# A hybrid decoder layer on one core: first weights through other tiles and in one chain, and the norm of the linear attention in four VectorE operations a piece

## The chip, the core and the metric

The kernel runs on one core of one Trainium2 chip. The metric is device time in microseconds (us). The engines are TensorE (PE; PEld is its weight load), VectorE (DVE), ScalarE (ACT), GpSimd (POOL) and SyncE (SP), which here issues every DMA. Each engine works through its own list of instructions in order and waits on semaphores where an operand or a buffer is not ready.

## What is computed

The reference is one decoder layer for 1024 tokens of width 1024. Cut to what matters here:

```python
h = rmsnorm(x, norm_mix)
proj = h @ w_in          # q, kv, gates of the sparse attention; q, k, v, rank, r of the linear one; merge gates
k_cmp, v_cmp = compress_blocks(...)
o_a = nsa_attention(...)                         # compressed, selected and sliding-window branches
o_b = gla_chunked(q_gla * GLA_DK ** -0.5, k_gla, v_gla, log_a)
o_b = rmsnorm(o_b, gla_norm)                     # over the 128 values of each head
o_b = o_b * silu(r_gla)
merged = gate_a * (o_a @ w_up_nsa) + gate_b * (o_b @ w_up_gla)
x = x + merged @ w_out
x = x + (silu(rmsnorm(x) @ w_ffn_gate) * (rmsnorm(x) @ w_ffn_up)) @ w_ffn_down
return rmsnorm(x, norm_final)
```

`rmsnorm(x, g)` is `x * rsqrt(mean(x*x) + 1e-6) * g`.

## The kernel before

Everything is kept transposed: 128 features on the partitions, tokens along the row, in halves of 512 tokens. Each float32 operand is split into a high and a low part, and each product is three matmuls (high by high, high by low, low by high). A weight's split has two steps: ACT copies it to the high part (`wh`, L353), then another engine subtracts (`wl`, L354; POOL for the projections' weights).

PE's order is the order in which the program is written. The other engines' lists are set by a scheduler with its own estimate of time, from priorities and from which buffers are free; DMAs of the first loads are kept in the order written (`load`, L481).

**The first stretch.** For each of eight blocks `k` of 128 features the loop from L484 loads both halves of `xT` and the weights `w_s` (queries and half of the keys of the linear attention). These weights pass through the tile `wf`, of which there are two, and which every later weight of the projections uses too. ACT makes `hh`, the high part of the scaled input (L498), DVE the low part `hl` (L501). ACT squares the input in place (L508) and POOL adds the squares up in `ssq` (L510, six times); DVE adds the last block (L527). ACT and DVE split that sum into `ssh` and `ssl` (L530, L531). PE meanwhile does the products of all eight blocks into six PSUM banks, two of them of the tag `m` (L365 to L367). ACT then copies these two banks out as `qg` (L542), which frees them, and PE goes on with the second half of the keys, job `w_t[3]`, in the tag `m` (L404). After its first two blocks comes `first_roots` (L544): four matmuls with `ssh` and `ssl`, then the reciprocal root `rbc`. The jobs of the compressed keys and values follow (`work = dense([j0, ...])`, L710); the weights of job `n+1` are loaded while job `n` runs.

**The norm of the linear attention** (from L945) comes later, in eight pieces of one head and 512 tokens. SP loads the piece `tz`; ACT squares it and takes the high part (L953, L954), POOL the low part (L955). PE sums over the partitions with `onesr`, a tile of ones (L967). `rms_root` (L424) then runs ACT's Ln and Exp (L427, L429) beside four DVE operations (L428, L430, L431, L432), and two more DVE operations apply the gain and `silu(r)` (L971, L972). Between pieces PE works off the query jobs and one gate job from the `fill` queue; their banks of the tag `m` (two) are freed by DVE's `scaled` (L524).

Of the kernel before, what the change touches and what calls it, by code (L numbers as in the profile page):

```python
# [10 lines left out]
F32 = mybir.dt.float32  # L11
F32R = mybir.dt.float32r
BF = mybir.dt.bfloat16
U8 = mybir.dt.uint8
AF = mybir.ActivationFunctionType
OP = mybir.AluOpType
# [223 lines left out]
def layer_kernel(ctx, tc, a, outT):  # L240
# [33 lines left out]
    def ps_t():  # L274
        return bank("t")
# [12 lines left out]
    def big(nm, dt=F32, shape=(1024,)):  # L288
        return sb.tile([128, *shape], dt, name=nm, tag="c", bufs=NBIG)
# [28 lines left out]
    cmul = mcst.tile([128, 64], F32, name="cmul")  # L318
    ones = cst.tile([128, 128], F32, name="ones")
    onesr = cst.tile([128, 128], F32R, name="onesr")  # L320
    identb = mcst.tile([128, 128], BF, name="identb")
    mdb = mcst.tile([128, 128], BF, name="mdb")
    meb = mcst.tile([128, 128], BF, name="meb")
# [7 lines left out]
    def load_consts():  # L331
        load(ident, a["consts"][:, CI:CI + 128])
        load(tri, a["consts"][:, CTRI:CTRI + 128])
        load(cmul, a["consts"][:, CMUL:CMUL + 64])
        load(ggain, a["gla_norm"])
        load(w2b, a["gla_w2b"])
        V.tensor_copy(identb, ident)
        t = big("cst1")
        load(t[:, :768], a["consts"][:, CMD:CMD + 768])
        V.tensor_copy(mdb, t[:, 0:128])  # L340
        V.tensor_copy(meb, t[:, 128:256])
        V.tensor_copy(cmb.rearrange("p b n -> p (b n)"), t[:, 256:768])
        t = big("cst2")
        load(t[:, :64 * NLV], a["consts"][:, CLEV:CLEV + 64 * NLV])
        V.tensor_copy(lev.rearrange("p b n -> p (b n)"), t[:, :64 * NLV])


    def part(src, wh, wl, eng=None, wf=None):

        n = src.shape[1]  # L350
        wf = (wpool.tile([128, 512], F32, name="wf", bufs=2) if wf is None else wf)[:, :n]
        SP.dma_start(wf, src)
        S.activation(wh, wf, AF.Copy)  # L353
        (eng or V).tensor_tensor(wl, wf, f(wh), OP.subtract)  # L354

    def half_weights(src, o):

        n = min(4, src.shape[1] - o)
        wh = wpool.tile([128, 4, 128], F32R, name="wh", bufs=3)
        wl = wpool.tile([128, 4, 128], F32R, name="wl", bufs=3)  # L360
        part(*[t.rearrange("p a b -> p (a b)") for t in (src[:, o:o + n, :], wh[:, :n, :], wl[:, :n, :])], eng=P)
        return wh, wl

    def three(ps, wh, wl, xh, xl, first, last):
# [4 lines left out]
    def dense(jobs, two=True, per=1, ready=None):  # L369

        w, out = dict(ready or {}), []

        def load(n, o):
            if n < len(jobs) and o < jobs[n][0].shape[1] and (n, o) not in w:
                w[n, o] = half_weights(jobs[n][0], o)

        def at(n):
            def getw(k):  # L380
                wh, wl = w[n, k // 4 * 4]
                return wh[:, k % 4, :], wl[:, k % 4, :]
            return getw

        out += [(0.0, lambda: load(0, 0)), (0.0, lambda: load(0, 4))]
        for n in range(len(jobs)):
            items = jobs[n][1](at(n))
            cut = (len(items) // 2 if two else 0) + 4 * per
            out.append((0.0, lambda n=n: load(n + 1, 0)))
            out += items[:cut]  # L390
            out.append((0.0, lambda n=n: load(n + 1, 4)))
            out += items[cut:]
        return out
# [30 lines left out]
    def rms_root(st, n, denom, r, tmp=None):  # L424

        v, q = [t[:, :n] for t in tmp or (tiny("nv", 32), tiny("nq", 32))]
        S.activation(q, st[:, :n], AF.Ln, scale=1.0 / denom, bias=eps)  # L427
        V.tensor_scalar(v, st[:, :n], -0.5 / denom, -0.5 * EPS, op0=OP.mult, op1=OP.add)  # L428
        S.activation(q, q, AF.Exp, scale=-0.5)  # L429
        V.tensor_mul(v, v, q)  # L430
        V.tensor_mul(v, v, q)  # L431
        V.scalar_tensor_tensor(r, v, 1.5, q, op0=OP.add, op1=OP.mult)  # L432
# [21 lines left out]
    def log_exp():  # L454

        tc.keep_in_program_order(S.preload_act_table_set("natural_log_exp_and_others"))
# [7 lines left out]
    V.memset(ones, 1.0)  # L464
    V.memset(eps, EPS)
    V.tensor_copy(onesr, ones)
    log_exp()

    warm = prob("warm", BF)[:, :512]
# [14 lines left out]
    for k in range(NK):  # L484
        if k % 2 == 0:
            wh2, wl2 = big("w0h", F32R, (2, 512)), big("w0l", F32R, (2, 512))
        xf, wf = big("xf"), wpool.tile([128, 512], F32, name="wf", bufs=2)[:, :384]
        th, tl = row("hh", F32R), row("hl", F32R)
        wh, wl = wh2[:, k % 2, :384], wl2[:, k % 2, :384]
        with tc.high_priority():  # L490
            load(xf[:, hs(0)], a["xT"][:, k, hs(0)])
            if k == 0:
                load(gains, a["gains"])
            load(wf, a["w_s"][:, k, :])
            load(xf[:, hs(1)], a["xT"][:, k, hs(1)])
            for hf in range(2):
                x, hi = xf[:, hs(hf)], th[:, hs(hf)]
                S.activation(hi, x, AF.Copy, scale=gains[:, 0, k:k + 1])  # L498
                if hf == 0:
                    S.activation(wh, wf, AF.Copy)  # L500
                V.scalar_tensor_tensor(tl[:, hs(hf)], x, gains[:, 0, k:k + 1], f(hi), op0=OP.mult, op1=OP.subtract)  # L501
                if hf == 0:
                    (P if k > 1 else V).tensor_tensor(wl, wf, f(wh), OP.subtract)
        w0.append((wh, wl))
        if k == 0:
            S.activation(ssq, xf, AF.Square)
        else:
            S.activation(xf, xf, AF.Square)  # L508
            if k < NK - 1:
                P.tensor_add(ssq, ssq, xf)  # L510
        hh.append(th)
        hl.append(tl)
    load_consts()
    hhf = [[t[:, hs(hf)] for t in hh] for hf in range(2)]
    hlf = [[t[:, hs(hf)] for t in hl] for hf in range(2)]
# [4 lines left out]
    def scaled(dst, ps, hf, s=None):  # L520
        if s is None:
            V.tensor_mul(dst, ps, rbc[:, hs(hf)])
        else:
            V.scalar_tensor_tensor(dst, ps, s, rbc[:, hs(hf)], op0=OP.mult, op1=OP.mult)  # L524
# [33 lines left out]
    def proj(evac, bank=ps_m, fine=False):  # L558

        def make(getw):  # L560
            out = []
            for hf in range(2):
                out += products(getw, bank, hhf[hf], hlf[hf], 0,
                                lambda p, hf=hf: evac(p, hf), fine)
            return out
        return make

    fill = Fill()
    work = dense([(a["w_t"][3], proj(lambda p, hf: scaled(kg[hf][:, 1, :], p, hf)))])
    fill.add(work[:5] + [(900.0, first_roots)] + work[5:] + [(400.0, root_turned)])  # L570
    fill.flush()


    kc = mcst.tile([128, NG, 2, 64], F32, name="kc")
# [86 lines left out]
    def key_job(br):  # L661
        def evac(p, hf):
            if hf == 0:
                ks[br] = [big(f"ks{br}{g}", F32R) for g in range(NG)]
            rc, rs = mid("rc"), mid("rs")
            SP.dma_start(rc, a["rope"][:, 0, hs(hf)])
            SP.dma_start(rs, a["rope"][:, 1, hs(hf)])
            kt, sw = mid("krt"), mid("ksw")
            scaled(kt, p, hf)
            V.stream_shuffle(sw, kt, swap)  # L670
            V.tensor_mul(kt, kt, rc)
            V.tensor_mul(sw, sw, rs)
            V.tensor_add(kt, kt, sw)
            for g in range(NG):
                r, o = slice(64 * g, 64 * g + 64), slice(64 - 64 * g, 128 - 64 * g)
                k = ks[br][g]
                S.activation(k[r, hs(hf)], kt[r, :], AF.Copy)
                V.tensor_tensor(k[o, hs(hf)], kt[r, :], f(k[r, hs(hf)]), OP.subtract)
        return a["w_t"][6 + br], proj(evac)
# [16 lines left out]
    def token_proj(parts, ncol, evac, after={}):  # L696
        for b in range(NB):
# [6 lines left out]
            for fn in after.get(b, []):  # L704
# [2 lines left out]
    j0, h0, t0, s0 = compress_job(0)  # L707
    j1, h1, t1, s1 = compress_job(1)
    lb, wb = token_weights(a["w_b"], 512, 2)
    work = dense([j0, key_job(0), j1, key_job(1)])  # L710
    fill.add(work[:30] + h0 + work[30:41] + t0 + work[41:45] + s0 + work[45:51] + lb[:1] + work[51:56] + lb[1:2] + work[56:66]
             + h1 + lb[2:] + work[66:])
    fill.flush()

    vs = [big(f"vs{i}", F32R, (2, 4, 128)) for i in range(4)]
# [244 lines left out]
    for n, (h, hf) in enumerate(pieces):  # L960
        if n + 1 < len(pieces):
            ahead.append(squares(*pieces[n + 1]))
        fill.run(4400)
        tz, *parts = ahead.pop(0)
        ps = ps_t()
        for i, t in enumerate(parts):
            PE.matmul(ps, onesr, t, start=i == 0, stop=i == 1)  # L967
        nv, nq = mid("nv"), mid("nq")
        rms_root(ps, 512, float(GDV), nq, [nv, nq])
        t = tz[:, 0, :]  # L970
        V.scalar_tensor_tensor(t, t, ggain, nq, op0=OP.mult, op1=OP.mult)  # L971
        V.tensor_mul(t, t, tz[:, 1, :])  # L972
        SP.dma_start(ob2[:, h, hs(hf)], t)
# [764 lines left out]
```

## Time and profile before

| | before |
|---|---|
| three runs | 1654.77, 1650.31, 1653.8 us (median 1653.8) |
| the profiled execution | 1651.47 us, of which the span is 1649.6 us |
| PE busy | 1583.9 us (96%) |
| DVE, ACT, POOL busy | 1070.0, 809.7, 752.0 us |

The span runs from the first to the last instruction. A matmul's row shows its length in the pipeline; the next one starts before it ends. "[4.71 <-ACT qg L542]" behind a row means that the engine stood idle for 4.71 us before it and that ACT's instruction at L542 ended the wait. In the window rows the granted clock of PE is a share of full speed: 1.00 is 2.4 GHz, 0.50 is 1.2 GHz.

### The profile page before, as it was taken

How to read it: one execution, taken by the hardware profiler on the slowest of the kernel's cores; microseconds unless marked ns; L12 is line 12 of the kernel's file. 1: busy time of each engine (PE TensorE's matmuls, PEld its weight loads, DVE VectorE, ACT ScalarE, POOL GpSimd, SP SyncE). 2: the span in 40 equal slices, each digit the busy share in tenths (PEclk: the TensorE clock that was granted, in tenths of full speed). 3: DMA queues.
4: the chain of work that ended last, by engine and by line, in shares of the span. 5: the costliest groups of instructions: out<-in, count | busy, mean ns of one | idle time of the engine just before them, and what ended most of it. 6: DMA issues, size and time to landing. Idle time of an engine off the chain costs nothing.

```text
span 1649.6 us, 23202 instructions
## 1 busy us (share of the span) xinstructions
PE 1583.9 (96%) x8079; PEld 1314.8 (80%) x8079; DVE 1070.0 (65%) x1759; ACT 809.7 (49%) x1633; POOL 752.0 (46%) x668
## 2 busy tenths in 40 slices
PE   9899999998999999998898989999999999999997
PEld 6788978876888878886777778888888888888886
DVE  7771487695777787778655476744444444489776
ACT  6231466543676666767644344433334333444542
POOL 6210376664234442345124450356665666545560
PEclk9999999999999999999999999999999999999999
DMA  5331212342111111113256551333332333595414
GB/s 175 116 105 46 72 61 74 114 140 74 43 45 43 58 46 42 45 43 103 85 175 212 195 170 45 102 101 108 119 102 97 101 103 102 209 378 153 142 47 144
DMA packets 107208, 178.82 MB, mean 108 GB/s; under 512 B 11969, under 2 KB 26706, under 8 KB 107090
## 3 DMA queue, kind: packets, MB, share of 16 engines
q1 hardware_dynamic: 103778, 171.30, 31.7%
q10 hardware_dynamic: 3312, 6.03, 1.0%
q8 instruction: 64, 1.05, 0.3%
q14 instruction: 54, 0.44, 0.1%
HBM read 129.84 MB, written 47.45 MB: 107 GB/s over the span
## 4 chain that ended last, share of the span: by engine, by line
PE 75%; DVE 9%; DMA 5%; issue 4%; ACT 4%; POOL 3%; SPq 0%; DVEq 0%; ACTq 0%; POOLq 0%
PE m L404 11%; PE m L1352 9%; PE m L1353 9%; PE d L404 9%; PE m L1354 9%; PE m L1667 4%; PE m L1668 4%; PE m L1669 4%; PE t L1133 3%; PE o L1142 3%; PE s L1055 2%; PE s L1056 2%; POOL wl L354 1%; DMA wf<-in_w_out 1%; DVE qs L1004 1%
## 5 line engine op out<-in xcount | busy, mean ns | idle before, releaser
L354 POOL TENSOR_TENSOR wl<-wf,wh 128x512 fp32r<-128x512 f32 x106 | 145.6, 1375 | 319.0 <-ACT wh L353 297.8
L1352 PE MATMUL m<-xt,wh 128*128 128x512 f32 x412 | 161.4, 392 | 2.6 <-ACT sc L1358 2.6
L1354 PE MATMUL m<-xt,wl 128*128 128x512 f32 x412 | 160.3, 389 | 0.0
L1353 PE MATMUL m<-xt,wh 128*128 128x512 f32 x412 | 160.3, 389 | 0.0
L1284 POOL TENSOR_TENSOR wl<-ws,wh 128x512 fp32r<-128x512 f32 x76 | 107.4, 1418 | 91.0 <-ACT wh L1283 71.6
L1111 DVE TENSOR_TENSOR ptl<-t,pth 128x512 fp32r<-128x512 f32 (+1 forms) x168 | 99.5, 597 | 47.4 <-ACT pth L1110 46.0
L1284 POOL TENSOR_TENSOR wl<-wr,wh 128x512 fp32r<-128x512 f32 x69 | 92.4, 1339 | 57.9 <-ACT wh L1283 56.9
L353 ACT ACTIVATE wh<-wf 128x512 fp32r<-128x512 f32 x106 | 66.4, 628 | 98.7 <-PE m L404 38.9
L1283 ACT ACTIVATE wh<-wr 128x512 fp32r<-128x512 f32 x87 | 54.9, 631 | 120.4 <-POOL wl L1284 84.0
L404 PE MATMUL m<-hh,wh 128*128 128x512 f32 x240 | 103.8, 433 | 10.0 <-DVE qr L524 5.3
L1284 POOL TENSOR_TENSOR wl<-wd,wh 128x512 fp32r<-128x512 f32 x56 | 82.4, 1474 | 61.5 <-ACT wh L1283 58.0
L1667 PE MATMUL m<-xb,wh 128*128 128x512 f32 x280 | 109.3, 390 | 0.0
L1669 PE MATMUL m<-xb,wl 128*128 128x512 f32 x280 | 108.9, 389 | 0.0
L1668 PE MATMUL m<-xb,wh 128*128 128x512 f32 x280 | 108.9, 389 | 0.0
L1110 ACT ACTIVATE pth<-t 128x512 fp32r<-128x512 f32 (+1 forms) x168 | 87.6, 526 | 38.4 <-PE t L1133 35.3
L1284 DVE TENSOR_TENSOR xb<-ar,xb 128x512 fp32r<-128x512 f32 (+1 forms) x84 | 81.3, 984 | 35.2 <-ACT xb L1283 35.2
L1283 ACT ACTIVATE wh<-ws 128x512 fp32r<-128x512 f32 x76 | 47.9, 630 | 111.9 <-PE m L1353 95.2
L404 PE MATMUL m<-hh,wl 128*128 128x512 f32 x240 | 95.8, 399 | 1.1 <-POOL wl L354 1.1
L404 PE MATMUL m<-hl,wh 128*128 128x512 f32 x240 | 95.8, 399 | 0.0
L1352 PEld LDWEIGHTS m<-xt,wh 128*128 128x128 f32 x412 | 77.3, 188 | 22.2 <-ACT sc L1358 6.4
L1133 PE MATMUL t<-ident,p 128*128 128x128 f32 x528 | 83.6, 275 | 11.2 <-DVE ptl L1111 10.0
L1354 PEld LDWEIGHTS m<-xt,wl 128*128 128x128 f32 x412 | 77.3, 188 | 16.2
(381 smaller groups left out, 4674.1 us busy)
## 6 DMA issues: line engine op xcount, KB each, us to landing
ar<-actd SPq DMA_DIRECT2D x70, 256.0 KB, 3.0
wf<-in_w_t SPq DMA_DIRECT2D x58, 256.0 KB, 2.8
wr<-in_w_gate SPq DMA_DIRECT2D x44, 256.0 KB, 2.6
wr<-in_w_upf SPq DMA_DIRECT2D x44, 256.0 KB, 2.7
zd<-zt SPq DMA_DIRECT2D x40, 256.0 KB, 2.0
wd<-in_w_down SPq DMA_DIRECT2D x33, 256.0 KB, 5.2
wf<-in_w_out SPq DMA_DIRECT2D x32, 256.0 KB, 3.2
actd<-t SPq DMA_DIRECT2D x30, 256.0 KB, 2.5
```

The costliest lines, as they stand in the source:

```text
L354: (eng or V).tensor_tensor(wl, wf, f(wh), OP.subtract)
L404: PE.matmul(st["p"], w, x, start=k + i == 0, stop=k == n - 1 and i == 2)
L1111: V.tensor_tensor(tl[:, :c], pt[:, :c], f(th[:, :c]), OP.subtract)
L1133: PE.transpose(pt[:, bs(2 * b + par)], self.p[par][:, bs(kb + b)], ident)
L1283: S.activation(th, src, AF.Copy)
L1284: eng.tensor_tensor(tl, src, f(th), OP.subtract)
L1352: PE.matmul(ps, wh[:, c], xh, start=first and k == 0, stop=False, skip_group_check=not first)
L1353: PE.matmul(ps, wh[:, c], xl, start=False, stop=False, skip_group_check=not first)
L1354: PE.matmul(ps, wl[:, c], xh, start=False, stop=k == MH - 1, skip_group_check=not first)
L1667: PE.matmul(dst, wh[:, c], xh, start=first and p == 0, stop=False, skip_group_check=not first)
L1668: PE.matmul(dst, wh[:, c], xl, start=False, stop=False, skip_group_check=not first)
L1669: PE.matmul(dst, wl[:, c], xh, start=False, stop=p == NP - 1, skip_group_check=not first)
```

## The change

Four things change. The weights `w_s` pass through `ws`, a tile of the pool of ten middle tiles. The two halves of the weights of job `w_t[3]` are loaded by the same ordered list as the first loads, right after them and ahead of the constants. That job is put at the head of the chain of jobs that follows, with `first_roots` and `root_turned` (L552) at the same places in PE's order. And the norm of the linear attention uses a tile `meanr` of -1/128, so that the bank holds minus the mean; ACT takes Ln, Exp and a Square, and DVE four operations.

```diff
+    meanr = mcst.tile([128, 128], F32R, name="meanr")
...
-    def part(src, wh, wl, eng=None, wf=None):
+    def part(src, wh, wl, eng=None, wf=None, dma=SP.dma_start):
...
-        SP.dma_start(wf, src)
+        dma(wf, src)
...
+    V.tensor_scalar(meanr, ones, -1.0 / GDV, None, op0=OP.mult)
...
-        xf, wf = big("xf"), wpool.tile([128, 512], F32, name="wf", bufs=2)[:, :384]
+        xf, wf = big("xf"), mid("ws")[:, :384]
...
+    first = {(0, o): half_weights(a["w_t"][3], o, load) for o in (0, 4)}
     load_consts()
...
-    work = dense([(a["w_t"][3], proj(lambda p, hf: scaled(kg[hf][:, 1, :], p, hf)))])
-    fill.add(work[:5] + [(900.0, first_roots)] + work[5:] + [(400.0, root_turned)])
-    fill.flush()
...
-    work = dense([j0, key_job(0), j1, key_job(1)])
-    fill.add(work[:30] + h0 + work[30:41] + t0 + work[41:45] + s0 + work[45:51] + lb[:1] + work[51:56] + lb[1:2] + work[56:66]
-             + h1 + lb[2:] + work[66:])
+    work = dense([(a["w_t"][3], proj(lambda p, hf: scaled(kg[hf][:, 1, :], p, hf))), j0, key_job(0), j1, key_job(1)], ready=first)
+    fill.add(work[:5] + [(900.0, first_roots)] + work[5:20] + [(400.0, root_turned)] + work[20:48] + h0 + work[48:59] + t0
+             + work[59:63] + s0 + work[63:69] + lb[:1] + work[69:74] + lb[1:2] + work[74:84] + h1 + lb[2:] + work[84:])
...
-            PE.matmul(ps, onesr, t, start=i == 0, stop=i == 1)
+            PE.matmul(ps, meanr, t, start=i == 0, stop=i == 1)
         nv, nq = mid("nv"), mid("nq")
-        rms_root(ps, 512, float(GDV), nq, [nv, nq])
+        S.activation(nq, ps, AF.Ln, scale=-1.0, bias=eps)
+        S.activation(nq, nq, AF.Exp, scale=-0.5)
+        S.activation(nv, nq, AF.Square, scale=float(np.sqrt(0.5)))
+        V.scalar_tensor_tensor(nv, ps, EPS, nv, op0=OP.subtract, op1=OP.mult)
+        V.scalar_tensor_tensor(nq, nv, 1.5, nq, op0=OP.add, op1=OP.mult)
```

How the lists move. On POOL at the end of the first stretch, before (`w0l` is the low part of the last `w_s`, `ssq` the last sum of squares, `wl` the weights of `w_t[3]` and what follows):

```order
L510 TENSOR_TENSOR ssq<-ssq,xf 128x1024
L503 TENSOR_TENSOR w0l<-wf,w0h 128x384
L510 TENSOR_TENSOR ssq<-ssq,xf 128x1024
L354 TENSOR_TENSOR wl<-wf,wh 128x512 x7
L630 MEMSET hd 128x256
```

and now:

```order
L512 TENSOR_TENSOR ssq<-ssq,xf 128x1024
L505 TENSOR_TENSOR w0l<-ws,w0h 128x384
L355 TENSOR_TENSOR wl<-wf,wh 128x512 x2
L512 TENSOR_TENSOR ssq<-ssq,xf 128x1024
L355 TENSOR_TENSOR wl<-wf,wh 128x512 x5
L630 MEMSET hd 128x256
```

Two `wl`, those of `w_t[3]`, moved ahead of the last sum of squares. On ACT at the same place, before (`wh` is a weight's high part, `ssh` that of the sum of squares, `qg` the two copies that free the banks):

```order
L508 ACTIVATE xf<-xf 128x1024
L353 ACTIVATE wh<-wf 128x512 x2
L530 ACTIVATE ssh<-ssq 128x512 x2
L353 ACTIVATE wh<-wf 128x512
L542 ACTIVATE qg_255<-m 128x512
L542 ACTIVATE qg_256<-m 128x512
```

and now:

```order
L354 ACTIVATE wh<-wf 128x512 x2
L510 ACTIVATE xf<-xf 128x1024
L354 ACTIVATE wh<-wf 128x512
L533 ACTIVATE ssh<-ssq 128x512 x2
L545 ACTIVATE qg_269<-m 128x512
L545 ACTIVATE qg_270<-m 128x512
```

The third weight's high part moved from behind `ssh` to ahead of it; `qg` still stands behind `ssh`. On DVE, whose list also has the last `hl` now ahead of `identb` and the four `vc`, a stretch of the norm before (`nv`, `nq` are the norm's tiles, `qr` frees a bank of the query jobs):

```order
L524 SCALAR_TENSOR_TENSOR qr_2882<-m,rbc 128x512
L971 SCALAR_TENSOR_TENSOR tz<-tz,ggain,nq 128x512
L972 TENSOR_TENSOR tz<-tz 128x512
L428 TENSOR_SCALAR nv<-t 128x512
L430 TENSOR_TENSOR nv<-nv,nq 128x512
L431 TENSOR_TENSOR nv<-nv,nq 128x512
L432 SCALAR_TENSOR_TENSOR nq<-nv,nq 128x512
L971 SCALAR_TENSOR_TENSOR tz<-tz,ggain,nq 128x512
L524 SCALAR_TENSOR_TENSOR qr_2883<-m,rbc 128x512
```

and now:

```order
L527 SCALAR_TENSOR_TENSOR qr_2884<-m,rbc 128x512
L977 TENSOR_TENSOR tz<-tz 128x512
L973 SCALAR_TENSOR_TENSOR nv<-t,nv 128x512
L974 SCALAR_TENSOR_TENSOR nq<-nv,nq 128x512
L976 SCALAR_TENSOR_TENSOR tz<-tz,ggain,nq 128x512
L977 TENSOR_TENSOR tz<-tz 128x512
L527 SCALAR_TENSOR_TENSOR qr_2885<-m,rbc 128x512
```

Two operations fewer stand between one release of a bank and the next.

## Rows read from the trace of the kernel before

**Rows 1.** Stages: us, busy of PE, PEld, DVE, ACT, POOL (instructions), clock, DMA.

```profile
45.44:51.14 5.70, 5.70 (x14) 4.45 (x15) 1.06 (x2) 2.29 (x4) 0.81 (x1) 0.50 0.64 209
...
323.00:395.00 72.00, 65.62 (x276) 52.30 (x275) 54.78 (x72) 28.14 (x53) 39.41 (x29) 0.95 0.40 128
...
377.40:382.20 4.80, 4.79 (x11) 3.78 (x12) 4.66 (x8) 0.00 (x0) 0.00 (x0) 0.50 0.34 109
...
395.00:1649.60 1254.60, 1210.65 (x6114) 1004.09 (x6112) 808.33 (x1308) 632.80 (x1313) 575.37 (x467) 0.99 0.33 111
```

**Rows 2.** Timeline of PE around 40 us: start, us, instruction, [idle before <-releaser].

```profile
40.34 0.39 PE L367 MATMUL t<-hh,w0l 128*128 128x512 f32 x1
45.44 0.79 PE L404 MATMUL m<-hh,wh 128*128 128x512 f32 x1 [4.71 <-ACT qg L542]
```

**Rows 3.** Timeline of ACT, 36 to 46 us.

```profile
38.11 1.06 ACT L508 ACTIVATE xf<-xf 128x1024 f32<-128x1024 f32 x1 [5.11 <-DVE hl L501]
...
40.53 1.15 ACT L530 ACTIVATE ssh<-ssq 128x512 fp32r<-128x512 f32 x2 [0.32 <-DVE ssq L527]
44.27 0.63 ACT L353 ACTIVATE wh<-wf 128x512 fp32r<-128x512 f32 x1 [2.58 <-DMA wf<-in_w_t]
44.80 1.07 ACT L542 ACTIVATE qg<-m 128x512 f32<-128x512 f32 x2
```

**Rows 4.** The chain that ended last, 40 to 46 us: start, us, what.

```profile
41.66 2.59 DMA wf<-in_w_t
```

**Rows 5.** Timeline of POOL, 33 to 46 us.

```profile
33.10 1.47 POOL L503 TENSOR_TENSOR w0l<-wf,w0h 128x384 fp32r<-128x384 f32 x1
34.53 2.39 POOL L510 TENSOR_TENSOR ssq<-ssq,xf 128x1024 f32<-128x1024 f32 x1
39.77 3.54 POOL L354 TENSOR_TENSOR wl<-wf,wh 128x512 fp32r<-128x512 f32 x2 [2.84 <-ACT wh L353]
```

**Rows 6.** Timeline of DVE, 33 to 44 us.

```profile
33.62 1.03 DVE L337 CAST identb<-ident 128x128 bf16<-128x128 f32 x1
34.57 2.84 DVE L649 TENSOR_SCALAR vc<-ident 128x128 fp32r<-128x128 f32 x4
37.34 0.73 DVE L501 SCALAR_TENSOR_TENSOR hl<-xf,gains,hh 128x512 fp32r<-128x512 f32 x1
...
39.27 1.23 DVE L527 TENSOR_TENSOR ssq<-ssq,xf 128x1024 f32<-128x1024 f32 x1 [0.29 <-ACT xf L508]
41.20 2.65 DVE L531 TENSOR_TENSOR ssl<-ssq,ssh 128x512 fp32r<-128x512 f32 x2 [0.70 <-ACT ssh L530]
```

**Rows 7.** Waits, 323 to 395 us: total us, times, longest us.

```profile
PE m L404 <- DVE qr L524: 5.3, 3, 4.4
...
PE m L404 <- POOL wl L354: 1.1, 1, 1.1
```

**Rows 8.** Timeline of PE at 377 us.

```profile
377.41 0.77 PE L404 MATMUL m<-hh,wh 128*128 128x512 f32 x1 [4.43 <-DVE qr L524]
```

**Rows 9.** DVE by line and shape, 323 to 395 us: count, busy us, mean ns, idle before.

```profile
L431 DVE TENSOR_TENSOR nv<-nv,nq 128x512 f32<-128x512 f32 x8 | 8.4, 1044 | 0.2
L430 DVE TENSOR_TENSOR nv<-nv,nq 128x512 f32<-128x512 f32 x8 | 8.3, 1033 | 0.5
...
L524 DVE SCALAR_TENSOR_TENSOR qr<-m,rbc 128x512 f32<-128x512 f32 x8 | 5.5, 682 | 9.3 <-PE m L404 9.3
L428 DVE TENSOR_SCALAR nv<-t 128x512 f32<-128x512 f32 x8 | 5.4, 680 | 0.0
```

**Rows 10.** ACT by line, 323 to 395 us.

```profile
L953 ACT ACTIVATE sq<-tz 128x512 f32<-128x512 f32 x8 | 5.0, 629 | 16.1 <-DMA tz<-obd 13.6 <-DVE nv L428 2.4
```

**Rows 11.** Timeline of DVE in the norm, from 328 us.

```profile
329.79 0.69 DVE L430 TENSOR_TENSOR nv<-nv,nq 128x512 f32<-128x512 f32 x1
...
333.67 1.67 DVE L972 TENSOR_TENSOR tz<-tz 128x512 f32<-128x512 f32 x1
```

**Rows 12.** Timeline of POOL at the same time.

```profile
333.05 1.74 POOL L354 TENSOR_TENSOR wl<-wf,wh 128x512 fp32r<-128x512 f32 x1
```

More of the change, by code (lines that the diff above doesn't have):

```diff
@@ L345, in load_consts, with half_weights @@
         V.tensor_copy(lev.rearrange("p b n -> p (b n)"), t[:, :64 * NLV])
-    def part(src, wh, wl, eng=None, wf=None):
+    def part(src, wh, wl, eng=None, wf=None, dma=SP.dma_start):
         n = src.shape[1]
         wf = (wpool.tile([128, 512], F32, name="wf", bufs=2) if wf is None else wf)[:, :n]
-        SP.dma_start(wf, src)
+        dma(wf, src)
         S.activation(wh, wf, AF.Copy)
         (eng or V).tensor_tensor(wl, wf, f(wh), OP.subtract)
-    def half_weights(src, o):
+    def half_weights(src, o, dma=SP.dma_start):
         n = min(4, src.shape[1] - o)
@@ L360, in half_weights @@
         wl = wpool.tile([128, 4, 128], F32R, name="wl", bufs=3)
-        part(*[t.rearrange("p a b -> p (a b)") for t in (src[:, o:o + n, :], wh[:, :n, :], wl[:, :n, :])], eng=P)
+        part(*[t.rearrange("p a b -> p (a b)") for t in (src[:, o:o + n, :], wh[:, :n, :], wl[:, :n, :])], eng=P, dma=dma)
         return wh, wl
```

## The prediction, made before the changed kernel was run

> **What bounds the kernel now.** I began with the busy shares: PE 96%. So only what shortens or removes PE's own waits, or a slow clock behind them, counts. I then listed PE's waits over the two stretches that the change touches, and for each wait read the lists of the engine that ended it.
>
> In the first stretch PE ends its products with the matmul that starts at 40.34 and starts the next job at 45.44, after 4.71 us of waiting for ACT's `qg` [rows 2]. Until 51.14 it then runs at a granted clock of 0.50, the 1.2 GHz level [rows 1]. ACT was late because its list is in order: `qg` stands behind the high part of a weight of the job after next, which waited 2.58 us for its DMA [rows 3]. That DMA took 2.59 us from 41.66 [rows 4], and could start only when POOL's first `wl`, begun at 39.77, had freed the tile `wf` [rows 5]. The `wl` in turn waited for a copy on ACT that stood behind the square at 38.11, which waited 5.11 us for DVE's last `hl` [rows 3]. DVE had put that `hl` behind `identb` and four `vc` [rows 6].
>
> In the norm, 323 to 395 us, DVE is busy 54.78 of 72 us [rows 1], and PE waits three times for DVE to free a bank, 5.3 us together, the longest 4.43 at 377.41 [rows 7, 8]; behind that one the clock is at 0.50 for 4.80 us [rows 1]. A fourth wait, 1.1 us, is for POOL's `wl` [rows 7].
>
> **The change, first stretch.** Removed: the wait for `wf` in the loads, so the weights of `w_t[3]` land before they are wanted, and the DMA in the chain above starts earlier. What is late next? The lists of the changed program answer: `qg` still stands behind the two `ssh`, these need the sum of squares, and POOL's last addition to that sum now comes behind two `wl`. So I follow POOL and DVE from 33.10.
>
> The rows show that these two engines hold each other up. POOL's `wl` runs 333.05 to 334.79; DVE's product of two SBUF tiles, begun at 333.67, needs 1.67 us, where the same shape took 0.69 beside an idle POOL [rows 11, 12]. It ends at 335.34, 0.55 after POOL: it stood still and then ran. The cast `identb` took 1.03 us and ended when the `w0l` of 33.10 did (1.47), while the four `vc`, one tile in and one out, ran at 0.71 each beside POOL's 2.39 [rows 5, 6]. Both `ssl`, 2.65 us, fit too: they lie beside the two `wl` of 3.54 [rows 5, 6]. So I let the two engines take turns. The Trainium skill, page "SBUF — State Buffer", section "SBUF: two separate sides", says the same outright: the pair of ports that VectorE and GpSimd share is an exclusive lock, held for a whole instruction, and not a split of bandwidth. By that rule the sum below stands; by a split it would be the first rival's.
>
> The turns in the changed order: the `w0l` ends at 34.57. The last `hl`, now ahead, takes 0.55, to 35.1. The first `wl` takes 1.25 (3.54 for two, less the two waits of 0.5 for DVE's operations), to 36.35; `identb` 0.15; the second `wl` to 37.75; the last sum 2.39 [rows 5], to 40.1. That is 3.2 us later than the 36.92 of before. DVE runs the `vc` from 36.5, 2.84 [rows 6], to 39.3, and then has four casts, which took 0.9 between the end of the `hl` (38.07) and the wait of 0.29 before 39.27 [rows 6]; they stand still beside the sum until 40.1. The next `wl` on POOL, whose weight landed at about 39 (its tile is free at 36.35, and the DMA takes 2.59 [rows 4]), wants its turn at 40.1 too and takes 1.25 in between. Casts done at 42.3; DVE's addition 1.26 (39.27 to ACT's 40.53), two `ssh` 1.1, `qg` to PE's start 0.64 (44.80 to 45.44) [rows 2, 3]: PE starts at **45.2 to 45.3 instead of 45.44**, and its wait is as long as it was. I take a gain of **0.3** and leave the clock as it is.
>
> Bounds: if POOL's third `wl` comes behind the addition, 1.5 us gained; if the engines never hold each other, the sum ends at 33.10 + 1.2 + 2 x 1.27 + 2.39 = 39.2, and PE starts 3.0 us earlier at 42.4; if each turn costs one cast or one `wl` more, 0.8 lost. With a wait of 2 us the clock may stay up; 5.70 us at half clock are then worth up to half, 2.8 [rows 1].
>
> At nothing: `meanr`, one operation of 0.71 at most (a `vc`) before DVE's first `hl`, which waits for ACT; if that cover is gone it costs 0.7 once. The order of the loads: the two weight loads go ahead of seven loads of constants, which are first used behind them. From `first_roots` on all five lists are as before up to the norm, so that stretch only shifts.
>
> **The change, norm.** Of six DVE operations a piece four remain. The first, a product with one operand in PSUM, replaces L428; the row nearest to it is L524, the same form with a PSUM operand, 682 ns against 680 [rows 9]: no difference. L432 stays as it is. L430 and L431 go: 8.3 + 8.4 = 16.7 us of DVE's 54.78 [rows 1, 9]. If the waits for POOL in their means (1033 and 1044 ns, against 690 alone [rows 9, 11]) fall on the operations that remain, only 16 x 0.69 = 11.0 goes. Ahead of the wait at 377.41 stand 14 of the 16 removed, at least 14 x 0.69 = 9.7 us. PE will come there 1.95 us earlier (its waits before that, 0.9 for DVE and 1.1 for POOL), so 4.43 + 1.95 = 6.4 of the 9.7 are needed: the bank is free 3.3 us before PE asks, even at the low end. All 5.3 us of waits for DVE go [rows 7]. The slow clock behind them goes too: 4.80 us at half clock, worth 2.4 [rows 1]. Of POOL's 1.1 I take 0.3, since nothing in the change aims at it.
>
> ACT gets the Square, 8 x 0.63 = 5.0 us [rows 10], where it is busy 28.14 of 72 [rows 1]; it lies in the chain of a piece, in place of the two DVE operations that it replaces, so a piece takes no longer. Sum of the norm: 5.3 + 2.4 + 0.3 = **8.0** (bounds: 5.3 if the clock falls elsewhere, 8.8 with all of POOL's wait).
>
> Behind the norm the lists are equal again, and PE is busy 1210.65 of 1254.60 us [rows 1]: what PE gains early it keeps.
>
> **Sum**: 0.3 + 8.0 = 8.3. On the profiled execution: 1651.47 - 8.3 = 1643.2. The median of the three runs is 2.3 above that execution; I forecast from the median: 1653.8 - 8.3 = **1645.5 us**.
>
> **The rivals.** (1) The first stretch pays as well. For it: the wait for the DMA, 2.58 us, is truly gone, and the third `wl` may miss its turn. Against: the turns above. It gives 1.5 to 3.0 us and the clock: about 2.3 + 2.8 in place of 0.3, so 1640.7.
>
> (2) The norm's wait changes its name. ACT has a longer list, its `wh` stand behind Ln, Exp, Square and behind squares that wait 13.6 us for the DMA of `tz` [rows 10]; PE would wait for `wl` instead of for a bank, and with waits of 3 to 4 us the clock would fall as before. For it: that wait of 1.1 exists today. Against: the `tz` loads wait for stores that DVE now ends earlier. If 3 us of the 8 remain as gain: 1650.5.
>
> (3) Slower. The Square writes a tile of the pool of ten, which DVE must have left; if ACT stands there, the ten conversions of weights in the stretch stand behind it. Today the stretch loses 8.8 us; at 0.9 us of PE's wait for each conversion nothing is gained, and it decides from 1.4 us, 5 us slower than before. At 1.5: 15 - 8.8 - 0.3 = 5.9, 1659.7. Against: ACT is idle for 44 of 72 us.
>
> (4) The gain is given back behind the norm, since something other than PE sets the pace there: about 1652. Against: PE's busy time there, above.
>
> **How the numbers follow.** This kernel's runs can tell about 0.3%, 5 us, from no change. Forecast 0.50 (1643 to 1648); rival 1 0.22; rival 2 0.15; rival 3 0.06; rival 4 0.07. Faster by more than 5 us (below 1648.8): nearly all of the forecast (0.47), rival 1, and a little of rival 2 (0.03): 0.72. Within: 0.03 + 0.12 + 0.07 = 0.22. Slower: 0.06. The range takes in the forecast, rival 1 with its larger bound and the bound of 8.8 (down to 1637) and rival 2 (up to 1651).
>
> **What would show it.** In the changed profile PE's wait before the first job of the tag `m` should still be over 4 us and be ended by `qg`, now behind `ssh`, with the clock at 0.50 after it; a start before 44 us speaks for rival 1. DVE's busy time in the norm should be 38 to 44 us, no wait of PE for `qr` over 1 us, and the clock at 1.00 throughout. A PE wait for `wl` or `wh` over 2 us there speaks for rival 2 or 3. The forecast is wrong if the stretch behind the norm is not as long as before within 2 us.

## The result, and the profile after

The changed kernel takes 1643.35 us in the median of seven runs (1638.27 to 1646.98), the kernel before 1653.8; the ratio is 0.9934, with a 95% interval of 0.9912 to 0.9957. By the ratio that is 10.9 us less, between 7 and 15 (10.5 by the two medians), where 8.3 were forecast. The profiled execution took 1645.19 us, with a span of 1643.3.

PE's list is the same in both programs, so the same matmul can be looked up in both traces. Where it starts:

| the same matmul | before | after | shift |
|---|---|---|---|
| first job of the tag m | 45.44 | 45.24 | -0.2 |
| first of `root_turned` | 60.09 | 58.63 | -1.5 |
| first behind the wait for `krt` | 111.20 | 111.39 | +0.2 |
| one of a gate job, ahead of the norm | 322.92 | 324.17 | +1.2 |
| the last at the low clock of before | 382.23 | 373.13 | -9.1 |
| first behind a wait in the attention | 401.07 | 391.92 | -9.2 |
| end of the span | 1649.6 | 1643.3 | -6.3 |

The norm gained 10.3 us (from +1.2 to -9.1). The first stretch gained 1.5 and had lost it again before 111. Behind the norm (from -9.1 to -6.3) this execution lost 2.8.

**First stretch.** Timeline of PE, then windows (us, busy PE, PEld, DVE, ACT, POOL, clock, DMA), of the changed kernel:

```profile
45.24 0.80 PE L405 MATMUL m<-hh,wh 128*128 128x512 f32 x1 [4.34 <-ACT qg L545]
```

```profile
45.24:48.00 2.76, 2.76 (x7) 2.18 (x8) 0.28 (x1) 0.44 (x1) 0.00 (x0) 0.50 0.46 186
48.00:50.00 2.00, 2.00 (x10) 1.68 (x9) 0.52 (x1) 1.21 (x2) 0.00 (x0) 0.94 0.00 0
...
61.00:66.00 5.00, 5.00 (x16) 3.92 (x16) 4.25 (x13) 0.00 (x0) 0.00 (x0) 0.66 0.37 123
323.00:391.92 68.92, 67.28 (x303) 55.24 (x301) 43.36 (x62) 34.89 (x64) 41.82 (x35) 1.00 0.44 140
```

The wait is still there, for the same `qg` [rows 2], but the clock is back soon after 48 us instead of at 51.14 [rows 1]. Then it falls a second time, between 61 and 66 us, where before ran at 1.00 and where PE does not wait at all. That takes the 1.5 us back.

What set 45.24 are the lists of ACT, POOL and DVE (timelines of the changed kernel; the `vc` one by one):

```profile
39.13 0.63 ACT L354 ACTIVATE wh<-wf 128x512 fp32r<-128x512 f32 x1 [2.77 <-DMA wf<-in_w_t]
43.56 1.15 ACT L533 ACTIVATE ssh<-ssq 128x512 fp32r<-128x512 f32 x2 [3.80 <-DVE ssq L530]
44.62 1.06 ACT L545 ACTIVATE qg<-m 128x512 f32<-128x512 f32 x2
```

```profile
34.67 3.00 POOL L355 TENSOR_TENSOR wl<-wf,wh 128x512 fp32r<-128x512 f32 x2
37.63 2.39 POOL L512 TENSOR_TENSOR ssq<-ssq,xf 128x1024 f32<-128x1024 f32 x1
39.99 1.27 POOL L355 TENSOR_TENSOR wl<-wf,wh 128x512 fp32r<-128x512 f32 x1
```

```profile
35.18 1.32 DVE L338 CAST identb<-ident 128x128 bf16<-128x128 f32 x1
36.42 1.33 DVE L649 TENSOR_SCALAR vc<-ident 128x128 fp32r<-128x128 f32 x1
37.67 2.44 DVE L649 TENSOR_SCALAR vc<-ident 128x128 fp32r<-128x128 f32 x1
40.03 1.32 DVE L649 TENSOR_SCALAR vc<-ident 128x128 fp32r<-128x128 f32 x1
41.27 0.21 DVE L649 TENSOR_SCALAR vc<-ident 128x128 fp32r<-128x128 f32 x1
...
42.31 1.21 DVE L530 TENSOR_TENSOR ssq<-ssq,xf 128x1024 f32<-128x1024 f32 x1
```

Read the DVE and POOL rows against each other: `identb` ends as the first `wl` does, the first `vc` as the second, the second `vc` as the sum (40.02), the third as the third `wl` (41.26). The fourth, with nothing on POOL, takes 0.21 us. Each of these four fillers, 0.2 us for a `vc` alone, stood for one POOL instruction, and here the two engines went strictly by turns.

**Norm.** PE's waits between 323 and 392 us, and DVE by line:

```profile
PE o L1130 <- DVE ptl L1116: 1.6, 1, 1.6
```

```profile
L977 DVE TENSOR_TENSOR tz<-tz 128x512 f32<-128x512 f32 x8 | 8.4, 1055 | 0.2
L974 DVE SCALAR_TENSOR_TENSOR nq<-nv,nq 128x512 f32<-128x512 f32 x8 | 8.1, 1010 | 0.4
...
L973 DVE SCALAR_TENSOR_TENSOR nv<-t,nv 128x512 f32<-128x512 f32 x8 | 5.5, 688 | 2.9 <-ACT nv L972 2.9
L527 DVE SCALAR_TENSOR_TENSOR qr<-m,rbc 128x512 f32<-128x512 f32 x8 | 5.5, 685 | 9.4 <-PE m L405 9.4
```

The one wait left belongs to the attention. The waits for `qr` and for POOL's `wl` [rows 7] are gone, the clock is 1.00 throughout, and DVE is busy 43.36 us where it was 54.78 of a similar window [rows 1].

### The profile page after: what moved, and what is told of

It reads as the page before. It is cut to its first block, busy times and chain, and to the rows that moved or that the text cites. A ratio compares the mean times of both kernels' runs of the same rounds, so it can differ in the third digit from the quotient of the medians.

```text
span 1643.3 us, 23186 instructions
## 1 busy us (share of the span) xinstructions
PE 1587.8 (97%) x8079; PEld 1318.8 (80%) x8079; DVE 1053.8 (64%) x1744; ACT 814.6 (50%) x1641; POOL 749.9 (46%) x668
## 4 chain that ended last, share of the span: by engine, by line
PE 77%; DVE 8%; DMA 4%; issue 4%; ACT 3%; POOL 3%; SPq 0%; DVEq 0%; ACTq 0%; POOLq 0%
PE m L405 11%; PE d L405 9%; PE m L1357 9%; PE m L1358 9%; PE m L1359 9%; PE m L1672 4%; PE m L1673 4%; PE m L1674 4%; PE t L1138 3%; PE o L1147 3%; PE s L1060 2%; PE s L1061 2%; DMA wf<-in_w_out 2%; POOL wl L355 1%; POOL xx L796 1%
```

## The experiments

Kernels measured together share a chip and the runs of the kernel before: its median was 1653.71 beside `e1` to `e4`, 1652.36 beside `e5` to `e8`, and 1652.66 beside `e9` to `e11`. The changed kernel was not run again beside them, so a difference to it is given by the medians and, where that matters, by the ratios to the kernel before as well.

**Each part alone.** `e1_norm_alone` is the kernel before with `meanr` and the four operations; `e2_first_alone` is the changed kernel without them:

```diff
-            PE.matmul(ps, onesr, t, start=i == 0, stop=i == 1)
+            PE.matmul(ps, meanr, t, start=i == 0, stop=i == 1)
...
-        rms_root(ps, 512, float(GDV), nq, [nv, nq])
+        S.activation(nq, ps, AF.Ln, scale=-1.0, bias=eps)
...
```

> The kernel before with only the norm in four VectorE operations a piece (and the tile of -1/128). Theory: the norm carries the whole gain of the changed kernel. PE's waits in 323 to 395 us of before (6.4 us idle, of which 4.43 for qr) and the 4.8 us at half clock behind the longest go, 8.8 us, and some tenths for each of the four waits: 9 to 10 us less than before, 1643.5 to 1645; no wait of PE for qr over 1 us; the first stretch as in before (PE starts its job at 45.4, clock 0.50 to 51). Rival, the first stretch pays part: only 5 to 7 us less, 1647 to 1649.

> The kernel before with only the change of the first stretch (w_s through other tiles, early loads of w_t[3], one chain); the norm in six operations as before. Theory: PE starts its first job of the tag m at 45.2 to 45.3, 0.2 us earlier, behind a wait of over 4 us for qg; a clock that comes back sooner may add up to 1.7; so 1652 to 1654, within 0.3% of before, and the norm's wait for qr of about 4.4 us is there as before. Rival, the first stretch pays 3 us or more: 1648 to 1651.

The norm alone: 1641.74 (5 runs), ratio 0.9931 (0.9919 to 0.9944), which is 11.4 us less where 9 to 10 were expected. The first stretch alone: 1652.27 (11 runs), 0.9994 (0.9981 to 1.0006). The whole gain is the norm's; the first stretch moves nothing that the runs can tell. PE in both (of the first kernel, then of the second):

```profile
45.74 0.80 PE L405 MATMUL m<-hh,wh 128*128 128x512 f32 x1 [4.69 <-ACT qg L544]
```

```profile
45.31 0.50 PE L404 MATMUL m<-hh,wh 128*128 128x512 f32 x1 [4.35 <-ACT qg L543]
375.94 0.47 PE L404 MATMUL m<-hh,wh 128*128 128x512 f32 x1 [3.91 <-DVE qr L525]
```

In the trace of the norm alone the matmul at 382.23 of before starts at 372.05, 10.2 us earlier, and from there to the end of the span it takes 1267.4 us in both kernels. What PE gains in the norm is kept.

**The order on ACT.** `e3_qg_first` is the changed kernel with the two copies ahead:

```diff
-    for hf in range(2):
-        S.activation(ssh[:, hs(hf)], ssq[:, hs(hf)], AF.Copy)
...
     for n in range(2):
         S.activation(dst[n], acc[n], AF.Copy)
...
+    for hf in range(2):
+        tc.keep_in_program_order(S.activation(ssh[:, hs(hf)], ssq[:, hs(hf)], AF.Copy))
...
```

> The changed kernel with one thing moved: on ACT the two qg copies stand ahead of the two ssh, so the banks come free without the sum of squares. Theory: the late sum costs PE only through ACT's order. PE starts its job at about 41.0 instead of 45.24, does the six matmuls of two blocks, and then waits for ssl until 44.9 to 45.5; the four matmuls of the roots end near 46 instead of 49.0: 3 us less than the changed kernel, 1640, and up to 1 us more where the clock stays up. Rival, the roots and DVE's chain behind them set the pace in any case: less than 1 us, 1642.5 to 1644.

1636.66 (4 runs), ratio 0.9895 (0.9882 to 0.9909): 6.7 less than the changed kernel (6.4 by the ratios), more than the 3 to 4 expected. PE:

```profile
40.87 0.39 PE L405 MATMUL m<-hh,wh 128*128 128x512 f32 x1
...
44.41 0.50 PE L549 MATMUL o<-ssh,onesr 128*128 128x512 f32 x1 [2.02 <-ACT ssh L544]
45.13 0.50 PE L550 MATMUL o<-ssl,onesr 128*128 128x512 f32 x1 [0.22 <-DVE ssl L545]
```

The start, the wait for the roots and the place of the next matmul of the job (46.08 instead of 49.01) are as forecast, 2.9 us. The rest goes with the clock: in this trace, the fastest of the four runs, it is at 0.50 in four stretches ahead of the end, in the changed kernel's in ten (44.8 to 48.2, 61.9 to 65.3, and eight later). Why these fall where they do is not settled here.

**The sum first as well.** `e4_sum_and_qg_first` adds to this POOL's sum ahead of the `wl`, and a third buffer of `wf`; `e7_three_wf` and `e8_qg_first_three_wf` take this apart:

```diff
-        wf = (wpool.tile([128, 512], F32, name="wf", bufs=2) if wf is None else wf)[:, :n]
+        wf = (wpool.tile([128, 512], F32, name="wf", bufs=3) if wf is None else wf)[:, :n]
...
-        (eng or V).tensor_tensor(wl, wf, f(wh), OP.subtract)
+        (tc.keep_in_program_order if dma is load else lambda i: i)((eng or V).tensor_tensor(wl, wf, f(wh), OP.subtract))
...
-            if k < NK - 1:
+            if k < NK:
                 P.tensor_add(ssq, ssq, xf)
...
-    V.tensor_add(ssq, ssq, xf)
```

> The changed kernel with qg ahead of ssh on ACT, and in addition the sum of squares ahead of the two wl on POOL: POOL adds the last block too (DVE no longer does), the two wl of w_t[3] stand behind it, and the tile wf has three buffers so that the next weight's high part does not stand in ACT's way. By turns of DVE and POOL: w0l to 34.7, hl to 35.2, a sum to 37.6, the last sum to 40.1, ssh behind the two qg to 42.0, ssl by 43.4. Theory: PE starts at about 41.0 and its wait for ssl is at most 1 us; the roots are done near 44 instead of 49.0; 5 us less than the changed kernel and 1 more for the clock, 1637 to 1639. Rival, as for the kernel with qg alone first: under 1.5 us, since the chain behind the roots sets the pace; 1642 to 1644.

> The changed kernel with three buffers of the tile wf instead of two, and nothing else. The kernel with the sum and qg first had this too, and gained most of its 12.7 us behind 740 us of the span. Theory: it is the third buffer that pays there, since PE's waits for POOL's wl (7.2 us in the changed kernel, 4.9 in that one) and the low clock behind them shrink: 4 to 7 us less than the changed kernel, 1636 to 1639, with the wait before the job at 45 us unchanged. Rival, the low clock falls by chance: within 2 us of the changed kernel, 1641 to 1645.

> The changed kernel with qg ahead of ssh on ACT and three buffers of wf; the sum of squares stays behind the two wl on POOL as in the changed kernel. Theory: the earlier sum was worth nothing, because DVE's ssl stood behind casts and vc that took turns with POOL's wl (ssl at 45.0 us with the earlier sum, at 44.4 without it), so this one is as fast as the kernel with the sum first too: 1629.5 to 1632. Rival, the earlier sum paid 2 us or more: 1633 to 1635.

Sum, `qg` and third buffer: 1630.69 (0.9863, 0.9848 to 0.9878), 6 us below the 1637 to 1639 expected. Third buffer alone: 1635.58 (0.9892, 0.9874 to 0.9909). `qg` and third buffer, without the sum: 1631.34 (0.9873, 0.9856 to 0.989). So the third buffer alone gives 7.8 us (6.9 by the ratios) where 4 to 7 were expected, and on top of `qg` first 5.3: the two gains do not add up in full. The earlier sum gives 0.7, less than the runs can tell. The gain of `e4` belongs to `qg` and to `wf`. Its PE reached the job at 42.82, not at 41.0, since it had run at the low clock from 22.4 to 25.8, behind a wait of 2.29 us for `w0l`. Why the sum is worth nothing, DVE of that kernel:

```profile
38.01 5.06 DVE L649 TENSOR_SCALAR vc<-ident 128x128 fp32r<-128x128 f32 x4
42.98 1.32 DVE L341 CAST mdb<-cst 128x128 bf16<-128x128 f32 x1
...
45.01 1.28 DVE L545 TENSOR_TENSOR ssl<-ssq,ssh 128x512 fp32r<-128x512 f32 x2
```

The sum was done at 40.5, but `ssl`, expected by 43.4, stood behind fillers that still went by turns with POOL. Where the third buffer pays: between the same two matmuls, windows of the changed kernel and of the kernel with three buffers.

```profile
828.67:980.77 152.10, 144.65 (x607) 115.41 (x605) 86.20 (x97) 61.88 (x105) 71.55 (x51) 0.97 0.57 187
```

```profile
826.58:973.14 146.56, 140.41 (x606) 114.31 (x605) 82.19 (x98) 61.99 (x106) 70.79 (x52) 0.99 0.60 194
```

PE's waits for `wl` in the two windows, which the expectation named as the reason:

```profile
PE m L405 <- POOL wl L355: 6.6, 6, 2.8
```

```profile
PE m L405 <- POOL wl L355: 6.1, 4, 3.1
```

They shrink by 0.5 us, and all of PE's idle time by 1.3 (7.45 to 6.15). The other 4.2 of the 5.5 us is busy time, at a mean clock of 0.99 instead of 0.97. That the third buffer brings the gain is shown by the runs; how it does so is not.

**The fillers out of DVE's way.** `e10_fillers_on_act` is `e8` with the `vc` and three casts on ACT:

```diff
-                    V.tensor_scalar(v, ident, 0.0, None, op0=OP.mult)
+                    S.activation(v, ident, AF.Copy, scale=0.0)
...
-        V.tensor_copy(mdb, t[:, 0:128])
+        S.activation(mdb, t[:, 0:128], AF.Copy)
...
```

> The kernel with qg first and three wf, and the four vc and three of the four casts of the constants on ACT instead of DVE. It tests the turns: in the changed kernel each vc, 0.21 us alone, stood behind one POOL instruction (1.33, 2.44, 1.32 us). Without them ahead of it DVE's last addition waits for POOL's sum alone (done at about 40.1), or for one wl more, and the roots' first matmul comes 0.5 to 1.8 us earlier than 43.99. Theory: 0.5 to 2 us less than that kernel, 1629.3 to 1630.8. Rival, DVE's list there does not matter (the sum of squares itself or ACT is the limit): first matmul of the roots at 43.7 or later, 1631 to 1632.5.

DVE, then PE:

```profile
36.12 1.49 DVE L346 CAST lev<-cst 128x448 uint8<-128x448 f32 x1
39.90 2.30 DVE L530 TENSOR_TENSOR ssq<-ssq,xf 128x1024 f32<-128x1024 f32 x1 [2.29 <-POOL ssq L512]
```

```profile
42.91 0.49 PE L549 MATMUL o<-ssh,onesr 128*128 128x512 f32 x1 [0.99 <-ACT ssh L544]
```

The roots start 1.08 us earlier than in `e8` (43.99), as the turns say: DVE's addition now waits for POOL's sum alone and then for one `wl` (2.30 instead of 1.21). The time does not show it: 1631.66 (6 runs, 1627.09 to 1636.22; 0.9871, 0.9851 to 0.9891). One microsecond is less than these runs can tell.

**The early loads left out.** `e11_mended_without_early_loads` is `e1` with `qg` first and three `wf`, so without the changed kernel's first stretch.

> The kernel before with the norm in four operations, qg ahead of ssh on ACT, and three buffers of wf: the changed kernel's tiles for w_s, its early loads and its one chain are left out. Theory: once the order on ACT is mended, the changes of the first stretch are worth nothing: PE starts its job at 41 to 42 and the roots near 43 to 44.5, within 2 us of the kernel with qg first and three wf, 1629.5 to 1633. Rival, the early loads are needed: PE starts at 43.5 or later, 1634 to 1638.

1630.98 (0.9864, 0.9846 to 0.9882), as fast as `e8`; the roots' first matmul starts at 44.24. PE's first job starts at 42.87 and not at 41 to 42, behind a low clock from 21.2 to 24.6. Once ACT's order is mended and a third `wf` is there, the early loads, the tiles `ws` and the one chain are worth nothing that the runs can tell.

**How much relief the norm needed.** `e5_five_operations` moves the Square to DVE, `e6_square_twice` executes it twice on ACT:

```diff
-        S.activation(nv, nq, AF.Square, scale=float(np.sqrt(0.5)))
+        V.scalar_tensor_tensor(nv, nq, 0.5, nq, op0=OP.mult, op1=OP.mult)
```

> The changed kernel with the Square of the norm moved from ACT to VectorE: five DVE operations a piece instead of four. It asks how much of DVE's relief was needed. Of the operations ahead of the wait for qr at 377 us of before, 7 instead of 14 are then gone: by 0.69 us each 4.8 us, less than the 6.4 needed, so a wait of about 1.5 us comes back; by the means of 1.04 us 7.3, more than needed, so none does. Theory: between these, a wait for qr of 0 to 1.5 us and 0 to 2 us more than the changed kernel: 1643 to 1645.5. Rival, the relief was needed in full: a wait of 3 to 4 us and the clock at 0.50 behind it, 1647 to 1650.

> The changed kernel with ACT's Square of the norm executed twice, which doubles what the change adds to ACT there (5.0 us more in the stretch). Theory: ACT's list has room, no new wait of PE over 1 us from 318 to 390 us, within 1.5 us of the changed kernel: 1642 to 1645. Rival, ACT's operations stand ahead of the high parts of weights (wh) and PE pays: a wait for wl or wh of 2 us or more in that stretch, 1646 or more.

Five operations: 1648.32 (0.9977, 0.9966 to 0.9987), the Square twice: 1648.71 (0.9979, 0.9968 to 0.999). Both give back 5 us of the gain by the medians, 7 by the ratios. My times for both were wrong. The stretch of the norm itself, between the matmuls at 322.92 and 382.23 of before, takes 59.3 us before and 49.0 in the changed kernel; with five operations it takes 52.5, with the Square twice 56.2. PE's waits in the norm, of the one and of the other:

```profile
PE m L405 <- DVE qr L527: 1.3, 1, 1.3
PE m L405 <- POOL wl L355: 1.2, 1, 1.2
```

```profile
PE t L968 <- POOL ql L955: 3.4, 1, 3.4
PE m L405 <- DVE qr L527: 3.2, 1, 3.2
```

With five operations the wait for `qr` is what the low end of the estimate gave, 1.3 us against 1.5. What I had left out is a wait for `wl` beside it; this trace also has a low clock from 397.8 to 404.6, and a start of the first job that is 1.1 us later (46.35). With the Square twice the waits are larger, and ACT and DVE show why:

```profile
343.38 0.63 ACT L953 ACTIVATE sq<-tz 128x512 f32<-128x512 f32 x1 [3.96 <-DMA tz<-obd]
343.91 0.61 ACT L973 ACTIVATE nv<-nq 128x512 f32<-128x512 f32 x1
```

```profile
344.62 0.69 DVE L974 SCALAR_TENSOR_TENSOR nv<-t,nv 128x512 f32<-128x512 f32 x1 [3.71 <-issue]
```

The second Square (L973) came to stand behind the next piece's `sq` in six of the eight pieces. Here that `sq` waited 3.96 us for its DMA, and DVE's next operation stood until the Square was done. Is it this place, or the load of 5.0 us? `e9_other_square_twice` gives ACT the same load at `sq`; DVE's list stays as it is, and one operation on ACT and two on POOL change places:

```diff
-        S.activation(sq, tz[:, 0, :], AF.Square)
+        S.activation(sq, tz[:, 0, :], AF.Square); S.activation(sq, tz[:, 0, :], AF.Square)
```

> The changed kernel with the first Square of a piece (sq, of the loaded tz) executed twice. ACT gets the same 5.0 us more as in the kernel with the norm's own Square twice, but all other lists keep their order: there the repeated Square came to stand behind the next piece's sq, which waits for its DMA, and DVE waited up to 3.7 us for it. Theory: the place in ACT's list cost those 5 us, not ACT's load; this one is within 1.5 us of the changed kernel, 1642 to 1645, with no wait of PE over 1 us from 318 to 390 us. Rival, the load itself costs: 1647 or more and waits for ql or qr of 2 us or more.

1643.19 (4 runs; 0.9938, 0.9917 to 0.996), the time of the changed kernel, and no wait of PE over 0.2 us:

```profile
318.00:391.00 73.00, 72.47 (x335) 59.54 (x333) 42.60 (x62) 39.98 (x73) 41.90 (x35) 1.00 0.43 136
```

The stretch of the norm takes 49.4 us, 0.4 more than in the changed kernel. So the load costs next to nothing at this place. What cost `e6` 5.5 us more than `e9` (6.8 by the ratios) is the order that the other place brought. In `e6` a few DVE operations changed places as well, and their share was not taken apart.

## Why the prediction was right, step by step

**The norm carries the gain: right, its size 2 us short.** Forecast 8.0; the stretch between the matmuls at 322.92 and 382.23 of before is 10.3 us shorter, in the changed kernel as in the norm alone, whose runs gained 11.4 (9.3 to 13.4). Two terms were mis-sized. Of POOL's 1.1 us I took 0.3; all of it went. And the idle time of a wait is not the whole of it. At the first three waits of before (0.38, 0.47 and 1.10 us of idle time) the shift grows by 0.65, 0.75 and 1.38 from the matmul ahead of the wait to the second one behind it. PE of before at the first of them:

```profile
352.66 0.50 PE L404 MATMUL m<-hh,wh 128*128 128x512 f32 x1 [0.38 <-DVE qr L524]
352.99 0.40 PE L404 MATMUL m<-hl,wh 128*128 128x512 f32 x1
353.23 0.39 PE L404 MATMUL m<-hh,wl 128*128 128x512 f32 x1
```

A matmul's row is 0.39 long, while the next one in a running series starts after 0.23, so the idle time is counted from 0.16 too late; and the first one behind a wait is longer (0.50 here), which adds 0.1. At the fourth wait the shift grows by 4.59 for 4.43 of idle time, and the slow clock behind it by 2.3 where 2.4 was forecast. That makes 9.7; the other 0.6 is spread over matmuls that do not wait, and its cause stays open.

**DVE's relief: right.** The six operations of before take 46.5 us in all, the four of the changed kernel 29.7, so 16.8 went where 16.7 was forecast; the fear that the waits for POOL would fall on those that stay did not come true. Ahead of the wait at 377.41 the low end of the relief was right, but not the slack. DVE's `qr` of before, then the same `qr` and the matmul that asks for its bank in the changed kernel:

```profile
376.58 0.68 DVE L524 SCALAR_TENSOR_TENSOR qr<-m,rbc 128x512 f32<-128x512 f32 x1
```

```profile
367.90 0.68 DVE L527 SCALAR_TENSOR_TENSOR qr<-m,rbc 128x512 f32<-128x512 f32 x1
370.63 0.39 PE L405 MATMUL m<-hh,wh 128*128 128x512 f32 x1
```

Counted from the matmul at 322.92 of before (324.17 in the changed kernel), the bank is free 9.9 us earlier, where the low end gave 9.7. But PE asks 8.0 us earlier and not 6.4, since a wait that goes gives it more than the idle time. So the bank is free 2 us ahead, not 3.3. With five operations it is free 4.5 us earlier than before, where half of the low end gave 4.8.

**The first stretch gains nothing: right, on a wrong inner step.** The `hl` ended at 35.26 (forecast 35.1), the second `wl` at 37.67 (37.75), the sum at 40.02 (40.1), DVE's addition began at 42.31 (42.3) and PE at 45.24 (45.2 to 45.3). But I had the `vc` run beside POOL at 0.71 each and be done at 39.3, and the casts stand still. It was the first three `vc` that stood still, to 41.35, and the casts behind them ran freely. The 0.71 was a mean over a group of four [rows 6]. One by one the same group of before reads (timeline of DVE, first and last):

```profile
34.57 2.44 DVE L649 TENSOR_SCALAR vc<-ident 128x128 fp32r<-128x128 f32 x1
...
37.20 0.21 DVE L649 TENSOR_SCALAR vc<-ident 128x128 fp32r<-128x128 f32 x1
```

The first stood for POOL's whole sum of 2.39, the others took 0.2. The end came out right because the number of turns was: four POOL instructions (three `wl` and the sum) end between `hl` and the addition, whoever stands behind them. The Trainium skill, page "SBUF — State Buffer", section "Who interferes with whom", counts `tensor_scalar` and casts among the operations that can hold the shared ports, so by its list the `vc` could stand still; the traces agree, and I had read the row against it.

**The clock behind that wait: wrong.** Forecast 0.50 as long as before (5.7 us of PE's time); it was about 3. In all six traces with this first stretch and `qg` behind `ssh` the low clock there lasts 3.4 us (behind waits of 2.7 to 4.35 us), in the two of the old one 6.8 (4.7 us both times). In four of the six it falls again near 62 us, in the old ones never. The net is what `e2` shows: 1.0 us, with an interval from 3 faster to 1 slower. That nothing was left of it in the changed kernel's trace is in part luck: in the trace of `e2` the clock does not fall near 62 us, and the 1.4 us gained are still there at the matmul ahead of the norm (321.57 instead of 322.92).

**The stretch behind the norm.** It should have been as long as before within 2 us and was 2.8 longer in the profiled execution; by the prediction's own sign this step failed there. Its lists are the same; in this trace it has seven stretches at the low clock ahead of the end instead of three. In the norm alone it is equal to 0.1 us, so the norm's operations are not the cause. In `e2`, `e5`, `e6` and `e9`, which have the new first stretch, it is 3.0, 0.3, 0.5 and 2.4 longer, with four, four, five and five low stretches. So it is no fixed price, and the low clock alone does not explain it. Whether the new first stretch makes it likelier, five traces cannot tell.

**The rivals.** The first stretch did not pay (rival 1), the norm's wait did not change its name (rival 2), and the runs kept the norm's gain (rival 4). Rival 2's condition for the clock would not have held in `e6` either: behind its waits of 3.4 and 3.2 us in the norm the clock stayed at 1.00. Rival 3 was dismissed because ACT is idle most of the time. That reason is bad: `e6` shows that an operation placed behind one that waits for a DMA can cost 5 us or more, `e9` that the same load in another place costs next to nothing. The changed kernel is on the good side of it because its Square stands ahead of the next `sq`.

## What to carry to other kernels

Before a wait is attacked from its far end (earlier loads, more tiles), look at what stands between the release and the engine that gives it: here two copies moved ahead of two others on one in-order list were worth more (6.7 us) than all the loads and tiles (1.0, less than the runs can tell), and one more buffer of a small staging tile alone gave 7.8. Read rows of a repeated instruction one by one where another engine may hold it up, since a mean hides that one of four paid for all. Price a new operation by where it lands in its engine's list, above all whether a DMA wait stands ahead of it, and only then by its length.

## What the runs showed that was not expected

The clock does not follow the length of one wait. Before and after, PE waits the same at the same place and then runs at different clocks (timeline of PE and a window behind it, of before and then of the changed kernel):

```profile
218.59 0.71 PE L778 MATMUL o<-tri,lsg 128*128 128x128 f32 x4 [1.83 <-ACT kt L864]
```

```profile
219.00:222.00 3.00, 3.00 (x21) 2.57 (x21) 1.32 (x4) 1.18 (x4) 3.00 (x5) 1.00 0.58 197
```

```profile
218.77 1.12 PE L778 MATMUL o<-tri,lsg 128*128 128x128 f32 x4 [1.85 <-ACT kt L864]
```

```profile
219.00:222.00 3.00, 3.00 (x12) 2.71 (x12) 0.00 (x0) 1.17 (x4) 3.00 (x5) 0.50 0.59 211
```

With 1.83 us of idle time it stayed at 2.4 GHz, with 1.85 it went to 1.2 GHz; behind the 3.4 and 3.2 us of `e6` it stayed at 2.4 GHz. Near 62 us it fell with no wait at all, behind a stretch of short matmuls (`root_turned`, 16 of them in 1.94 us) that stands in both kernels. What decides between the two stays open. The spread of the changed kernel's runs goes roughly with the mean clock: the fastest of the seven (1638.27) has 0.993, the four slowest 0.988 to 0.989.
